# Order of a sum and a remainder, place of a bias load, of three normalisations and of an epsilon in a one-layer attention kernel

## The chip, the cores and the metric

The kernel runs on one core of one Trainium2 chip. A core has TensorE (PE; its weight loads are shown apart, as PEld), VectorE (DVE), ScalarE (ACT), GpSimd (POOL) and SyncE (SP), which here issues nearly all DMA transfers. The engines run side by side, each through its own instructions in a fixed order, and wait for each other by semaphores. The metric is the device time of one execution in microseconds, as the median of several runs.

## The reference

One layer of a streaming encoder, for a sequence of 1024 rows of width 1024, in float32. All matrices are real inputs; nothing is constant.

```python
mod = silu(c) @ w_ada + b_ada                      # shift, scale and gate, each 1024 wide
u = layer_norm(x) * (1 + scale) + shift
h = u @ w_in                                       # q, k, v, g of 8 FoX heads and of 8 stick-breaking heads, ff
log_f = log_sigmoid(ff + b_f);  f_cum = cumsum(log_f, axis=1)
# FoX heads: causal softmax(q k^T / 8 + f_cum[q] - f_cum[k]) @ v
# stick-breaking heads, strictly causal: exp(log_sigmoid(z) + sum of later log_sigmoid(-z)) @ v, z = q k^T / 8
y = concat(fox * silu(fg), sb * silu(sg)) @ w_out
resid = 2 ** 0.25 * x + gate * y
out = layer_norm(resid) * ln_g + ln_b              # epsilon 1e-5 in both norms
```

## The kernel before

Each factor of a product is split into a high half, rounded to TensorE's fast float32 type, and a low half, the remainder. A product is then three: high by high, low by high and high by low. In names, `hi` and `h` stand for high, `lo` and `l` for low.

The work goes in four stages. **The start** normalises the first four tiles of 128 rows of x, transposes them on PE, applies scale and shift, and multiplies the result with the first weights. **The late round** does the same with the last four row tiles. **Attention** goes through 8 pairs of heads with 16 units each (2 heads by 8 query blocks of 128 rows). The projections of the next pairs are spread between the units on PE. **The output** multiplies with `w_out` and normalises again, tile by tile.

Tile's scheduler sets the order of an engine by a simulated time, except where the code fixes it: PE and SP run in program order in the start (`tc.manual_schedule`), PE also afterwards. `after(...)` lets the instructions in its block be ordered only behind a given one, which sets an order and no wait. Buffers come from pools: a pool tag has a number of buffers, and a tile that asks for one waits until all users of the earlier tile in it are done. Tags that matter here: `att` (6 buffers: x_0 to x_5, then the gate weights `wg`, then attention's tiles), `ptl` (3: at first the weights `hw_5`, `hw_6`, `hw_7` of the start, later low halves of attention weights), `T` (2 PSUM banks, for transposes and short products) and `acc`, `pv`, `fl` for accumulators.

In the start, `kb` counts 8 blocks of 128 columns of x. For each, VectorE forms the scale and the shift from 512 KB of `w_ada` (`mod_term(kb, i)`, one sum for i = 0 and one for i = 1, each a product with row sums into `modc`). PE transposes (`u_turn`). ScalarE forms the high half (`u_high`) and the full value, in place in PSUM (`u_full`). VectorE forms the remainder `ul` (`u_rest`). The transposed block 1 lies in the bank that later accumulates `st_k1` (`acc0[NW]`); the others lie in a bank of their own, `xT_early`. The loads of w_ada have three buffers, so the load of block kb + 3 waits for the second sum of block kb. The weights of the start are split by ScalarE (high, `whi_st`) and POOL (low, `wlo_st`); both halves of a block must be there before PE multiplies with it.

`norm_stats(t)` takes mean and variance of row tile t on VectorE, and on POOL adds epsilon and raises to the power -1/2 (`ln_finish`). `norm_x(t)` then normalises in place, on ScalarE for t up to 5 and on VectorE for 6 and 7. Tiles 4 to 7 are first used by the transposes of `late_round(0)`.

`v_first(t, acc)` computes tile t of the v projection of pairs 0 and 1, in 24 products. ScalarE then copies two high halves out of PSUM and VectorE subtracts for the two low ones (`v_tile`). Tiles 0 and 2 use the two halves of one PSUM tile, `late_acc` (`st_late` in the trace), so the first product of tile 2 waits for the copies of tile 0.

The gate vector is `silu(c) @ w_ada` for the third part: POOL multiplies and adds eight loads `wg` in 16 halves (`gate_term`), and `gen_gate` sums over the partitions on PE, one product pair for each half of 512 columns into a `T` bank. VectorE adds the bias `bg`, which is loaded as one row repeated over all 128 partitions. `gen_gate` runs among the fillers of the first attention units, and its T banks alternate with those of attention's transposes (`T_0_0_0`, `T_0_0_1`).

In the output, `o_half` collects a row tile's sum and statistics; the last tile (`OUT_ORDER[-1]`, tile 1) does so in three pieces. After the last statistics, VectorE normalises columns 0 to 832, while POOL, ScalarE, POOL and VectorE in turn treat columns 832 to 1024.

Of the kernel before, what the change touches and what calls it, by code (L numbers as in the profile page):

```python
# [8 lines left out]
F32 = mybir.dt.float32  # L9
# [18 lines left out]
def tile_hybrid_layer(  # L28
# [27 lines left out]
    def att_tile(name, dt=F32):  # L56
        return big("att", 6, name, dt)
# [105 lines left out]
        nc.tensor.matmul(sc_all[:, kt // 4, kt % 4 * P:][:, :P], sc[:, kt:kt + 1].to_broadcast([P, P]), ident,  # L163
                         start=True, stop=True)

    powed = [None]

    def ln_finish(st, name):
        mv = sb.tile([P, 2], F32, tag="mv", bufs=3, name=f"mv_{name}")
        nc.vector.bn_aggr(mv, st)  # L170
        rs = sb.tile([P, 2], F32, tag="rs", bufs=3, name=f"rs_{name}")
        nc.gpsimd.tensor_scalar_add(rs[:, 0:1], mv[:, 1:2], EPS)
        powed[0] = nc.gpsimd.tensor_tensor(rs[:, 0:1], rs[:, 0:1], mhalf, op=ALU.pow)
        return mv, rs

    def ln_stats(src, name):
        st = sb.tile([P, 3, 6], F32, tag="st", bufs=3, name=f"st_{name}")[:, :2, :]
        nc.vector.bn_stats(st[:, 0, :], src[:, 0:512])
        nc.vector.bn_stats(st[:, 1, :], src[:, 512:1024])
        return ln_finish(st, name)  # L180
# [7 lines left out]

    def norm_stats(t):
        mv, rs = norm[t] = ln_stats(xt[t], f"a{t}")  # L190
        if t not in NORM_ON:
            nc.gpsimd.tensor_scalar(rs[:, 1:2], mv[:, 0:1], rs[:, 0:1], -1.0, op0=ALU.mult, op1=ALU.mult)

# [117 lines left out]
    def make_v(g):  # L311
        for p in (2 * g, 2 * g + 1):
            vt[p] = sb.tile([P, NB, 256], F32R, tag="v", bufs=3, name=f"v_{p}")

    def v_tile(g, t, acc, quarters):
        n = 264 if g == 1 else 256
        ts_ = slice(t * P, (t + 1) * P)
        for kt in range(NB):
            hi, lo = quarters[kt // 2]
            s = slice((kt % 2) * n, (kt % 2) * n + n)  # L320
            nc.tensor.matmul(acc[:, :n], u_hi[kt][:, ts_], hi[:, s], start=(kt == 0), stop=False)  # L321
            nc.tensor.matmul(acc[:, :n], u_lo[kt][:, ts_], hi[:, s], start=False, stop=False)  # L322
            nc.tensor.matmul(acc[:, :n], u_hi[kt][:, ts_], lo[:, s], start=False, stop=(kt == NB - 1))  # L323
            if kt == 3:
                yield
        for i in range(2):
            v4 = vt[2 * g + i].rearrange("p t (x c) -> p t x c", c=HD)
            a4 = acc[:, i * P:(i + 1) * P].rearrange("p (x c) -> p x c", c=HD)
            nc.scalar.copy(v4[:, t, 0::2, :], a4)
            nc.vector.tensor_tensor(v4[:, t, 1::2, :], a4, v4.bitcast(F32)[:, t, 0::2, :],  # L330
                                    op=ALU.subtract)
        if g == 1:
            nc.vector.tensor_tensor(fsb[:, :, t], acc[:, 256:264], bf_sb, op=ALU.add)
        yield
# [321 lines left out]
    for kb in range(NB):  # L656
        last = kb == NB - 1
        if last:
            start_steps(ALL[:2], acc0, kb)
            for n in range(2):  # L660
                evac_m(*START[n], 0, acc0[n])
            start_steps(ALL[2:], acc0, kb)
            break
        start_steps(ALL[:4], acc0, kb, parts=(0,))
        u_turn(kb + 1, tp=xt_early if kb else acc0[NW])
        with after(split_at["k", kb + 1][0]):
            high = u_high(kb + 1)
        if kb == 0:
            with after(high):
                start_split(("h", 0))  # L670
            high = split_at["h", 0][0]
        with after(high):
            u_full(kb + 1)
        sums = [mod_term(kb + 2, i) for i in range(2 if kb == 0 else 1)] if kb + 2 < NB else []
        with after(*sums):
            rest = u_rest(kb + 1)
        if 0 < kb < NB - 2:
            with after(rest):
                mod_term(kb + 2, 1)
        if kb == 0:  # L680
            start_steps(ALL[:4], acc0, kb, parts=(1,))
        else:
            if kb == 1:
                start_steps(ALL[4:], acc0, 0)
            start_steps(ALL[4:], acc0, kb, parts=(0,))
            start_steps(ALL, acc0, kb, parts=(1,))
        if kb + 2 < NB:
            start_split(("k", kb + 2))
        if kb == 2:
            start_split(("h", 1))  # L690
        if kb + 5 < NB:
            load_ss(kb + 5)
            if kb == 0:
                load_w4(6, 2)
        if kb == 2:
            for n in range(2):
                v0_load(n)
            load_x(4)
            for n in range(2, 4):
                v0_load(n)  # L700
            for t in range(5, NB):
                load_x(t)
        if kb == 5:
            with after(*split_at["k", NB - 1]):
                for n in range(4):
                    v0_split(n)
            norm_stats(4)
            norm_stats(5)
            norm_x(4)
            norm_x(5)  # L710
        if kb == 6:
            with after(rest):
                for t in (6, 7):
                    norm_stats(t)
                    norm_x(t)
            make_v(0)

    wg = {}
# [11 lines left out]
            nc.gpsimd.tensor_tensor(gate[:, s], gate[:, s], wg[kt][:, s], op=ALU.add)  # L730

    def gen_gate():
        b = att_tile("bg")
        nc.sync.dma_start(b, b_gate.to_broadcast([P, D]))
        parts = [pt_tile(0, f"gate_{x}") for x in range(2)]
        nc.scalar.copy(parts[0], gate)
        nc.gpsimd.tensor_tensor(parts[1], gate, parts[0].bitcast(F32), op=ALU.subtract)
        for _ in range(GATE):
            yield
        for h in range(2):  # L740
            s = slice(h * 512, h * 512 + 512)
            gp = t_tile(f"gate_{h}")
            for part in range(2):
                nc.tensor.matmul(gp, half.to_broadcast([P, P]), parts[part][:, s], start=(part == 0), stop=(part == 1))
            nc.vector.scalar_tensor_tensor(gate[:, s], b[:, s], 0.5, gp, op0=ALU.mult, op1=ALU.add)
            yield

    def late_round(kb):
# [7 lines left out]
    def v_first(t, acc):  # L756
        for _ in v_tile(0, t, acc, v0_w):
            pass

    v_first(0, late_acc[:, 0, :])  # L760
    v_first(1, t_tile("v_0_1"))
    v_first(2, late_acc[:, 1, :])
    late_round(0)
# [4 lines left out]
    for kb in range(NB):  # L768
        if kb + 2 < NB:
            rounded = late_round(kb + 2)  # L770
        start_steps(range(2), acc1, kb, 512, 1024)
        if kb < 4:
            load_gate(kb)
            gate_term(kb, 0)
            gate_term(kb, 1)
        if kb == 3:
            v0_w.update((n, fetch_w(f"v0_{n}b", w_v[0, n], 512)) for n in (2, 3))
            for kt in range(4, NB):
                load_gate(kt)
                gate_term(kt, 0)  # L780
                gate_term(kt, 1)
        if kb < len(evacs):
            n, h = evacs[kb]
            with after(*rounded):
                evac_m(*START[n], 0, acc0[n], (h,))
# [95 lines left out]
    def o_half(t, h):  # L881
# [3 lines left out]
        if h == 0:  # L885
# [4 lines left out]
        nc.vector.scalar_tensor_tensor(r[:, s], xr[:, s], ALPHA, o_acc[t, h][:, :s.stop - s.start],  # L890
                                       op0=ALU.mult, op1=ALU.add)
        nc.vector.bn_stats(st[:, h, :], r[:, s])
        if h == ng - 1:
            mv, rs = ln_finish(st, f"b{t}")
            cuts = ((0, 512), (512, 832)) if t == OUT_ORDER[-1] else ((0, 512), (512, 1024))
            for a, b in cuts:
                gain, bias = ((ps_ln[i][a // 512][:, :b - a] for i in range(2)) if ps_ln else
                              (lgb[0][:, i, a:b] for i in range(2)))
                nc.vector.scalar_tensor_tensor(r[:, a:b], r[:, a:b], mv[:, 0:1], gain,
                                               op0=ALU.subtract, op1=ALU.mult)  # L900
                nc.vector.scalar_tensor_tensor(r[:, a:b], r[:, a:b], rs[:, 0:1], bias,
                                               op0=ALU.mult, op1=ALU.add)
                nc.sync.dma_start(out[ts_, a:b], r[:, a:b])
            if t == OUT_ORDER[-1]:
                e = slice(832, 1024)
                nc.gpsimd.tensor_scalar(rs[:, 1:2], mv[:, 0:1], rs[:, 0:1], -1.0, op0=ALU.mult, op1=ALU.mult)
                nc.scalar.activation(r[:, e], r[:, e], AF.Identity, scale=rs[:, 0:1], bias=rs[:, 1:2])
                nc.gpsimd.tensor_tensor(r[:, e], r[:, e], lgb[0][:, 0, e], op=ALU.mult)
                nc.vector.tensor_tensor(r[:, e], r[:, e], ps_ln[1][1][:, 832 - 512:], op=ALU.add)
                nc.sync.dma_start(out[ts_, e], r[:, e])  # L910
# [183 lines left out]
```

## Time and profile before

| | |
|---|---|
| median of 3 runs | 686.94 us (686.88 to 687.93) |
| profiled execution | 687.67 us |
| its span, first to last instruction | 685.9 us |
| PE busy | 668.6 us, 97% of the span |
| DVE busy | 450.2 us, 66% |
| POOL busy | 427.0 us, 62% |
| ACT busy | 381.5 us, 56% |
| granted TensorE clock, mean | 0.998 of full speed |

The profile is of one execution. A timeline row gives the start in us, the duration in us, the engine, the line of the kernel, the operation, what it writes and reads by the program's names without numbers, the shape, and how often it came in a row. In square brackets stands the time that the engine stood idle just before, and what ended that. SPq is a transfer's issue on SP's queue, not the transfer. Matmul ends are modelled, so the start of the next one tells more than the end of the last. In the list of waits a row names who waited, for whom, the total in us, how often, and the longest.

### The profile page before, as it was taken

The numbers are of one execution on the slowest core, as the hardware profiler recorded it, in microseconds if no ns is written. First come the engines' busy times: TensorE is split into PE (matmuls) and PEld (weight loads), VectorE is DVE, ScalarE is ACT, GpSimd is POOL, SyncE is SP. The second block draws the span as 40 slices with busy tenths as digits, with TensorE's granted clock in tenths as the row PEclk, the third lists the DMA queues.
The fourth block names the chain that finished last, engine by engine and source line by source line (L and its number), as shares of the span: only waits on it lengthen the run. The fifth ranks groups of instructions, "written<-read, shape, count | busy, mean of one in ns | idle before, by whom it ended". The sixth has DMA issues, their size and how long they took to land.

```text
span 685.9 us, 11768 instructions
## 1 busy us (share of the span) xinstructions
PE 668.6 (97%) x4021; PEld 587.9 (86%) x4021; DVE 450.2 (66%) x914; ACT 381.5 (56%) x861; POOL 427.0 (62%) x558
## 2 busy tenths in 40 slices
PE   5999999999999999999999999999999999999996
PEld 4788888888998888889998888889988889888885
DVE  6785348767666676676675665666565767774645
ACT  5577447856667666575674564655565666531000
POOL 5558967656448665556388897877584364665411
PEclk9999999999999999999999999999999999999999
DMA  9966241012102111112144554454351288143301
GB/s 338 410 224 240 62 124 43 25 40 54 40 9 72 39 55 55 38 50 60 35 137 142 177 162 121 151 151 142 105 146 43 65 328 321 57 156 122 125 31 62
DMA packets 45036, 81.60 MB, mean 119 GB/s; under 512 B 5232, under 2 KB 18864, under 8 KB 44976
## 3 DMA queue, kind: packets, MB, share of 16 engines
q1 hardware_dynamic: 43536, 76.63, 34.2%
q10 hardware_dynamic: 1440, 4.21, 2.0%
q8 instruction: 32, 0.52, 0.3%
q14 instruction: 28, 0.23, 0.1%
HBM read 60.34 MB, written 16.29 MB: 112 GB/s over the span
## 4 chain that ended last, share of the span: by engine, by line
PE 85%; POOL 6%; DMA 4%; issue 2%; DVE 2%; ACT 1%; SPq 0%; POOLq 0%; DVEq 0%
PE m L266 10%; PE pv L487 10%; PE m L267 10%; PE m L268 10%; PE T L472 9%; PE S L422 5%; PE S L421 5%; PE o L877 4%; PE o L875 4%; PE o L876 4%; PE v L321 4%; PE v L322 4%; PE v L323 4%; POOL gate L730 2%; POOL wg L729 1%
## 5 line engine op out<-in xcount | busy, mean ns | idle before, releaser
L266 PE MATMUL m<-uh,whi 128*128 128x512 f32 x304 | 126.5, 416 | 0.0
L268 PE MATMUL m<-uh,wlo 128*128 128x512 f32 x304 | 119.8, 394 | 0.0
L267 PE MATMUL m<-ul,whi 128*128 128x512 f32 x304 | 119.8, 394 | 0.0
L475 DVE TENSOR_TENSOR pt<-T,pt 128x512 fp32r<-128x512 f32 (+2 forms) x192 | 100.5, 550 | 17.9 <-ACT pt L474 16.9
L455 POOL TENSOR_TENSOR be<-be,kp 128x127 f32<-128x127 f32 (+3 forms) x64 | 77.1, 1206 | 35.4 <-DVE kp L451 23.5
L474 ACT CAST pt<-T 128x512 fp32r<-128x512 f32 (+2 forms) x192 | 85.7, 480 | 16.0 <-PE T L472 12.3
L447 DVE TENSOR_TENSOR_SCAN kp<-kp,floor 128x512 f32<-128x512 f32 (+2 forms) x64 | 65.2, 1018 | 30.9 <-ACT kp L441 30.0
L487 PEld LDWEIGHTS pv<-pt,v 128*128 128x128 f32 (+1 forms) x640 | 77.2, 163 | 4.5 <-DVE pt L475 0.7
L487 PE MATMUL pv<-pt,v 128*128 128x256 f32 (+3 forms) x640 | 80.4, 272 | 0.5 <-DVE pt L475 0.5
L436 POOL TENSOR_SCALAR a<-a,l 128x1024 f32<-128x1024 f32 (+3 forms) x64 | 47.9, 749 | 39.6 <-DVE l L435 28.6
L434 ACT ACTIVATE a<-a,nm 128x1024 f32<-128x1024 f32 (+3 forms) x64 | 49.8, 778 | 34.5 <-DVE nm L428 33.4
L268 PEld LDWEIGHTS m<-uh,wlo 128*128 128x128 f32 x304 | 57.2, 188 | 13.5
L421 PE MATMUL S<-k,q 128*128 128x512 f32 (+5 forms) x192 | 66.6, 348 | 0.2 <-DVE nm L428 0.2
L422 PE MATMUL S<-kl,qz 128*128 128x512 f32 (+5 forms) x192 | 65.5, 343 | 0.0
L266 PEld LDWEIGHTS m<-uh,whi 128*128 128x128 f32 x304 | 57.4, 189 | 8.5 <-DVE kl L254 0.2
L267 PEld LDWEIGHTS m<-ul,whi 128*128 128x128 f32 x304 | 57.5, 189 | 7.9
L428 DVE CUSTOM_DVE_ANT_0 a<-S,fb 128x1024 f32<-128x1024 f32 (+3 forms) x64 | 48.3, 755 | 20.4 <-PE S L422 8.9
L508 POOL TENSOR_TENSOR ty<-ty,sg 64x256 f32<-64x256 f32 x64 | 47.5, 742 | 22.6 <-DVE ty L507 11.5
L441 ACT ACTIVATE kp<-S 128x128 f32<-128x128 f32 (+3 forms) x64 | 41.7, 651 | 31.7 <-PE S L422 28.4
L321 PE MATMUL v<-whi_v,uh 128*128 128x256 f32 (+1 forms) x192 | 56.1, 292 | 0.0
L399 ACT CAST qz<-q 64x128 fp32r<-64x128 f32 x128 | 37.4, 295 | 32.8 <-PE S L422 31.6
L322 PE MATMUL v<-whi_v,ul 128*128 128x256 f32 (+1 forms) x192 | 54.3, 283 | 0.0
(283 smaller groups left out, 1594.2 us busy)
## 6 DMA issues: line engine op xcount, KB each, us to landing
raw<-in_w_qkg_dram SPq DMA_DIRECT2D x38, 256.0 KB, 2.8
wss<-in_w_ss_dram SPq DMA_DIRECT2D x16, 512.0 KB, 8.4
x<-in_x_dram SPq DMA_DIRECT2D x8, 512.0 KB, 6.9
k<-k SPq DMA_DIRECT2D x32, 128.0 KB, 2.3
wg<-in_w_gate_dram SPq DMA_DIRECT2D x8, 512.0 KB, 4.6
raw_o<-in_w_out_dram SPq DMA_DIRECT2D x16, 256.0 KB, 3.0
fb<-f_dr ACTq DMA_DIRECT2D x8, 512.0 KB, 4.2
wo_dr<-whi_o SPq DMA_DIRECT2D x16, 256.0 KB, 2.8
```

What stands on the lines that cost most here:

```text
L266: nc.tensor.matmul(acc, hi[:, c], u_hi[kt][:, s], start=(kt == 0), stop=False)
L267: nc.tensor.matmul(acc, hi[:, c], u_lo[kt][:, s], start=False, stop=False)
L268: nc.tensor.matmul(acc, lo[:, c], u_hi[kt][:, s], start=False, stop=(kt == NB - 1))
L321: nc.tensor.matmul(acc[:, :n], u_hi[kt][:, ts_], hi[:, s], start=(kt == 0), stop=False)
L322: nc.tensor.matmul(acc[:, :n], u_lo[kt][:, ts_], hi[:, s], start=False, stop=False)
L421: nc.tensor.matmul(S[:, s, :w], qst[p][h][:, qs], kst[p][h][:, ks], start=True, stop=False)
L422: nc.tensor.matmul(S[:, s, :w], z, klo[p][:, ks], start=False, stop=True)
L447: scan = nc.vector.tensor_tensor_scan(rv, rv, floor[0][:, 512 - n:][:, ::-1], initial=0.0, op0=ALU.mult, op1=ALU.max)
L455: nc.gpsimd.tensor_tensor(be[:, :ke - 1], be[:, :ke - 1], kp[:, 1:ke], op=ALU.mult)
L474: nc.scalar.copy(hi[:, :n, qo:qo + P], t3)
L475: nc.vector.tensor_tensor(lo[:, :n, qo:qo + P], t3, hi.bitcast(F32)[:, :n, qo:qo + P], op=ALU.subtract)
L487: nc.tensor.matmul(acc[:m, q0:256], vt[p][:, kb, h * P:h * P + m], pt[:, kb % 4, q0:], start=start, stop=stop)
```

## The change

It makes four edits.

1. At block 0 of the start, VectorE forms the remainder of block 1 between the two sums of block 2, as it did at the later blocks (first sum, remainder, second sum). At block 6 the remainder is ordered behind the joined statistics of row tile 4.
2. `norm_x` of row tiles 5, 6 and 7 is ordered behind the copies of the first v tile.
3. The gate bias is loaded behind the last gate weights, in a buffer of the tag `ptl` instead of `att`.
4. At the last output tile, epsilon is added to the first piece's statistics (to its sum of squares, times 1024), and no more to the variance after the last piece.

```diff
-    powed = [None]
+    powed, joined = [None], {}
-    def ln_finish(st, name):
+    def ln_finish(st, name, with_eps=False):
         mv = sb.tile([P, 2], F32, tag="mv", bufs=3, name=f"mv_{name}")
-        nc.vector.bn_aggr(mv, st)
+        joined["last"] = nc.vector.bn_aggr(mv, st)
         rs = sb.tile([P, 2], F32, tag="rs", bufs=3, name=f"rs_{name}")
-        nc.gpsimd.tensor_scalar_add(rs[:, 0:1], mv[:, 1:2], EPS)
-        powed[0] = nc.gpsimd.tensor_tensor(rs[:, 0:1], rs[:, 0:1], mhalf, op=ALU.pow)
+        var = mv[:, 1:2]
+        if not with_eps:
+            var = rs[:, 0:1]
+            nc.gpsimd.tensor_scalar_add(var, mv[:, 1:2], EPS)
+        powed[0] = nc.gpsimd.tensor_tensor(rs[:, 0:1], var, mhalf, op=ALU.pow)
...
         mv, rs = norm[t] = ln_stats(xt[t], f"a{t}")
+        joined[t] = joined.pop("last")
...
-            nc.scalar.copy(v4[:, t, 0::2, :], a4)
-            nc.vector.tensor_tensor(v4[:, t, 1::2, :], a4, v4.bitcast(F32)[:, t, 0::2, :],
-                                    op=ALU.subtract)
+            v_last[:] = [nc.scalar.copy(v4[:, t, 0::2, :], a4),
+                         nc.vector.tensor_tensor(v4[:, t, 1::2, :], a4, v4.bitcast(F32)[:, t, 0::2, :],
+                                                 op=ALU.subtract)]
...
-        sums = [mod_term(kb + 2, i) for i in range(2 if kb == 0 else 1)] if kb + 2 < NB else []
+        sums = [mod_term(kb + 2, 0)] if kb + 2 < NB else [joined[4]]
         with after(*sums):
             rest = u_rest(kb + 1)
-        if 0 < kb < NB - 2:
+        if kb + 2 < NB:
             with after(rest):
                 mod_term(kb + 2, 1)
...
             norm_x(4)
-            norm_x(5)
         if kb == 6:
             with after(rest):
                 for t in (6, 7):
                     norm_stats(t)
-                    norm_x(t)
...
     def gen_gate():
-        b = att_tile("bg")
-        nc.sync.dma_start(b, b_gate.to_broadcast([P, D]))
...
-            nc.vector.scalar_tensor_tensor(gate[:, s], b[:, s], 0.5, gp, op0=ALU.mult, op1=ALU.add)
+            nc.vector.scalar_tensor_tensor(gate[:, s], bg[:, s], 0.5, gp, op0=ALU.mult, op1=ALU.add)
...
     v_first(0, late_acc[:, 0, :])
+    with after(*v_last):
+        for t in (5, 6, 7):
+            norm_x(t)
...
                 load_gate(kt)
                 gate_term(kt, 0)
                 gate_term(kt, 1)
+            bg = pt_tile(1, "bg", F32)
+            nc.sync.dma_start(bg, b_gate.to_broadcast([P, D]))
...
+        final = t == OUT_ORDER[-1]
+        if final and h == 0:
+            nc.gpsimd.tensor_scalar_add(st[:, 0, 2:3], st[:, 0, 2:3], EPS * D)
         if h == ng - 1:
-            mv, rs = ln_finish(st, f"b{t}")
+            mv, rs = ln_finish(st, f"b{t}", with_eps=final)
```

VectorE, in the start around the remainder of block 1 (`ISA` with `wss_2` is a sum of block 2 and its second row the read of the row sums, `ul_1` the remainder). Before:

```order
L203 ISA wss_2_161,modc_128<-sc_all_103,wss_2_161,bss_sb_98 128x1024
L203 ISA modc_128 128x1
L203 ISA wss_2_161,modc_128<-sc_all_103,wss_2_161,bss_sb_98 128x1024
L203 ISA modc_128 128x1
L228 TENSOR_TENSOR ul_1_121<-st_k1_140,uh_1_113 128x512
L203 ISA wss_3_211,modc_128<-sc_all_103,wss_3_211,bss_sb_98 128x1024
```

and now:

```order
L207 ISA wss_2_161,modc_128<-sc_all_103,wss_2_161,bss_sb_98 128x1024
L207 ISA modc_128 128x1
L232 TENSOR_TENSOR ul_1_121<-st_k1_140,uh_1_113 128x512
L207 ISA wss_2_161,modc_128<-sc_all_103,wss_2_161,bss_sb_98 128x1024
L207 ISA modc_128 128x1
L207 ISA wss_3_211,modc_128<-sc_all_103,wss_3_211,bss_sb_98 128x1024
```

The remainder has moved ahead of the second sum.

VectorE, from the end of the start to the second v tile (`v_0`, `v_1` from `st_late` are the copies of the first v tile, from `v_0_1` those of the second; `x_6`, `x_7` the normalisations; `kl` belongs to k). Before:

```order
L250 TENSOR_TENSOR kl_0_242<-st_k0_137,k_0_1_241 64x512
L170 BN_AGGR mv_a7_510<-st_a7_507 128x2
L330 TENSOR_TENSOR v_0_516<-st_late_544,v_0_516 128x2x64
L198 TENSOR_SCALAR x_6_363<-x_6_363,mv_a6_501,rs_a6_503 128x1024
L330 TENSOR_TENSOR v_1_517<-st_late_544,v_1_517 128x2x64
L330 TENSOR_TENSOR v_0_516<-v_0_1_573,v_0_516 128x2x64
L198 TENSOR_SCALAR x_7_365<-x_7_365,mv_a7_510,rs_a7_512 128x1024
L330 TENSOR_TENSOR v_1_517<-v_0_1_573,v_1_517 128x2x64
```

and now:

```order
L254 TENSOR_TENSOR kl_0_242<-st_k0_137,k_0_1_241 64x512
L336 TENSOR_TENSOR v_0_513<-st_late_541,v_0_513 128x2x64
L170 BN_AGGR mv_a7_508<-st_a7_505 128x2
L336 TENSOR_TENSOR v_1_514<-st_late_541,v_1_514 128x2x64
L202 TENSOR_SCALAR x_6_363<-x_6_363,mv_a6_500,rs_a6_502 128x1024
L202 TENSOR_SCALAR x_7_365<-x_7_365,mv_a7_508,rs_a7_510 128x1024
L336 TENSOR_TENSOR v_0_513<-v_0_1_573,v_0_513 128x2x64
L336 TENSOR_TENSOR v_1_514<-v_0_1_573,v_1_514 128x2x64
```

Both copies of the first v tile stand ahead of x_6 and x_7, and both of the second behind. On ScalarE `x_5` has moved in the same way from ahead of the two casts of the first v tile to behind them.

SP, from the last gate weights to the first attention units (`wg` gate weights, `k` the half-copies of k, `raw` weights). Before:

```order
L722 DMA wg_7_789<-in_w_gate_dram 128x1024
L248 DMA k_1_0_245<-k_1_0_245 64x512
L248 DMA k_1_1_246<-k_1_1_246 64x512
L248 DMA k_0_0_240<-k_0_0_240 64x512
L248 DMA k_0_1_241<-k_0_1_241 64x512
L121 DMA raw_1_2_0_1228<-in_w_qkg_dram 128x512
L121 DMA raw_1_2_1_1234<-in_w_qkg_dram 128x512
L248 DMA k_1_0_245<-k_1_0_245 64x512
L121 DMA raw_2_0_0_1557<-in_w_qkg_dram 128x512
L734 DMA bg_958<-in_b_gate_dram 128x1024
L248 DMA k_1_1_246<-k_1_1_246 64x512
L797 DMA bf_sb_941<-in_b_f_dram 128x8
```

and now:

```order
L726 DMA wg_7_789<-in_w_gate_dram 128x1024
L788 DMA bg_795<-in_b_gate_dram 128x1024
L252 DMA k_1_0_245<-k_1_0_245 64x512
L252 DMA k_1_1_246<-k_1_1_246 64x512
L252 DMA k_0_0_240<-k_0_0_240 64x512
L252 DMA k_0_1_241<-k_0_1_241 64x512
L121 DMA raw_1_2_0_1228<-in_w_qkg_dram 128x512
L121 DMA raw_1_2_1_1234<-in_w_qkg_dram 128x512
L252 DMA k_1_0_245<-k_1_0_245 64x512
L121 DMA raw_2_0_0_1557<-in_w_qkg_dram 128x512
L252 DMA k_1_1_246<-k_1_1_246 64x512
L804 DMA bf_sb_943<-in_b_f_dram 128x8
```

bg has moved from behind the weights of `raw_2_0_0` to right behind the last gate weights, past eight transfers. Two other pairs have changed places by themselves: on VectorE the joined statistics of tile 4 stand ahead of the remainder of block 7, and on POOL the rounding of the last v weights stands ahead of the last sum of the gate. At the end POOL has lost one step of 128x1 behind the last statistics and has one more ahead of them. Everything else stands as it did.

More of the change, by code (lines that the diff above doesn't have):

```diff
@@ L313, in make_v @@
             vt[p] = sb.tile([P, NB, 256], F32R, tag="v", bufs=3, name=f"v_{p}")
+    v_last = []
     def v_tile(g, t, acc, quarters):
```

## Prediction

> **What bounds the kernel now.** I read the page first, then PE's part of the waits, then the timeline around each wait that the diff touches. The page gives the busy time and, in its fourth part, the chain that ended last, by engine:
>
> ```profile
> span 685.9 us, 11768 instructions
> ...
> PE 668.6 (97%) x4021; PEld 587.9 (86%) x4021; DVE 450.2 (66%) x914; ACT 381.5 (56%) x861; POOL 427.0 (62%) x558
> ...
> PE 85%; POOL 6%; DMA 4%; issue 2%; DVE 2%; ACT 1%; SPq 0%; POOLq 0%; DVEq 0%
> ```
>
> PE is busy for 668.6 of 685.9 us and carries most of the chain. No other engine is above 66%. So the time changes only where PE's few gaps change, or behind PE's last product. The waits of PE, longest first, of nine rows the four that matter here:
>
> ```profile
> PE gate L744 <- DVE gate L745: 0.8, 1, 0.8
> PE T L472 <- DVE pt L475: 0.8, 1, 0.8
> ...
> PE st_k L583 <- DVE ul L228: 0.5, 1, 0.5
> ...
> PE st_late L321 <- DVE v L330: 0.2, 1, 0.2
> ```
>
> Three of them lie at lines that the diff moves: the second bias product of the gate, the first product into st_k, and the third v tile. The T row lies right behind them and is not touched. Between the last of these and the final tile PE runs almost without a gap and the order of every engine is as before, so time won in front should arrive at the end as it is.
>
> **Edit 1, order at block 0.** PE may not write st_k before VectorE has taken ul from it, since that bank served as scratch for the transposed block 1. The stretch:
>
> ```profile
> 18.10 0.75 ACT L221 ACTIVATE st_k<-st_k,modc 128x512 f32<-128x512 f32 x1
> ...
> 18.88 1.28 DVE L203 CUSTOM_DVE_ANT_0 wss<-sc_all,wss,bss_sb 128x1024 f32<-128x1024 f32 x1
> ...
> 20.09 0.69 DVE L228 TENSOR_TENSOR ul<-st_k,uh 128x512 fp32r<-128x512 f32 x1
> ...
> 20.82 0.19 PEld L583 LDWEIGHTS st_k<-uh,whi_st 128*128 128x128 f32 x1 [0.77 <-DVE ul L228]
> ...
> 20.92 0.62 ACT L569 CAST whi_st<-raws 128x512 fp32r<-128x512 f32 x1 [2.07 <-DMA raws<-in_w_qkg_dram]
> ...
> 21.62 1.30 POOL L571 TENSOR_TENSOR wlo_st<-raws,whi_st 128x512 fp32r<-128x512 f32 x1 [2.05 <-ACT whi_st L569]
> ...
> 23.26 0.19 PEld L583 LDWEIGHTS st_q<-uh,wlo_st 128*128 128x128 f32 x1
> ```
>
> ScalarE is done with st_k at 18.85. VectorE then runs the second sum of block 2 for 1.28 us before ul. With the two exchanged, ul ends near 19.57, and the weight load that waited 0.77 us need not wait. The sum ends about 0.6 later, near 20.8. Its reader, the rounding of block 2, comes behind the cast of 20.92 to 21.54 on ScalarE, which waits for weights from memory, so this costs nothing while that load is no faster. SP also waits for that sum before it reloads the buffer, and so sends two loads and the 512 KB behind them 0.6 us later. Their users are sums two and a half blocks on, behind which VectorE stands idle for ScalarE; I take that as hidden.
>
> The 0.77 is not kept. The low halves of block 2's weights are made by 22.92 (21.62 and 1.30) from the same load, which does not move. PE loads them at 23.26. With the 0.04 us that passed between ul's end (20.78) and PE's load, PE can come forward by 23.26 - 22.92 - 0.04 = 0.30 us and no more. The ends are 0 (that load later) and 0.77 (earlier); I take **0.30**, the nearest row.
>
> The join of tile 4's statistics ahead of ul at block 6 falls into a gap in which VectorE waits for ScalarE. Its follower on POOL stands behind a weight split there, in the same order as before. I take 0, and it costs nothing either.
>
> **Edit 2, the last x tiles behind the first v tile.** Here are the first v tile's products, the third's, and what lies between:
>
> ```profile
> 49.19 0.29 PE L323 MATMUL st_late<-v_w,uh 128*128 128x256 f32 x1
> 49.31 0.28 PE L321 MATMUL v<-v_home,uh 128*128 128x256 f32 x1
> ...
> 49.71 1.24 ACT L199 ACTIVATE x<-x,rs_a 128x1024 f32<-128x1024 f32 x1
> 49.82 0.69 DVE L250 TENSOR_TENSOR kl<-st_k,k 64x512 fp32r<-64x512 f32 x1
> ...
> 50.98 0.27 ACT L329 CAST v<-st_late 128x128 fp32r<-128x128 f32 x1
> ...
> 52.06 0.29 PE L323 MATMUL v<-v_w,uh 128*128 128x256 f32 x1
> 52.20 0.28 DVE L330 TENSOR_TENSOR v<-st_late,v 128x128 fp32r<-128x128 f32 x1
> ...
> 52.54 0.39 PE L321 MATMUL st_late<-v_home,uh 128*128 128x256 f32 x1 [0.20 <-DVE v L330]
> ...
> 52.89 0.80 DVE L198 TENSOR_SCALAR x<-x,mv_a,rs_a 128x1024 f32<-128x1024 f32 x1
> ...
> 55.51 1.03 PE L211 MATMUL xT<-ident,x 128*128 128x128 f32 x8
> ```
>
> Products of this size start 0.12 apart (49.19, 49.31). The third tile's first would follow at 52.18 and starts at 52.54, when the second copy out of the first tile (52.20 to 52.48) is done: 0.36 us lost. What delays that copy is x_5's normalisation on ScalarE (1.24 us) ahead of the casts, and x_6's on VectorE. With both moved behind, ScalarE casts at 49.71, VectorE is free at 50.51, and the four short steps of about 0.28 with their handovers end near 51.4, about 0.8 before PE asks. So **0.36**, ends 0 and 0.36. Against it stands what is late next: x_5, x_6 and x_7 start behind that and end by about 53.2, with some 0.5 more if POOL's power for x_7 is slow. x_7 ended at 53.69 until now and the transposes want it at 55.51 less the 0.66 that PE gained. The copies of the second v tile move behind x_7 too, to about 54, and the second four transposes need their buffer near 55.2. Both are covered, by some 1 us.
>
> **Edit 3, the gate bias with the gate weights.** The bias load, the two bias products and what stands behind them:
>
> ```profile
> 81.89 0.40 PE L586 MATMUL st_q1b<-ul,hw 128*128 128x512 f32 x1
> ...
> 85.34 1.58 SPq L121 DMA_DIRECT2D raw<-in_w_qkg_dram  x2
> ...
> 91.90 0.45 SPq L734 DMA_DIRECT2D bg<-in_b_gate_dram  x1
> ...
> 93.22 0.41 POOL L455 TENSOR_TENSOR be<-be,kp 128x127 f32<-128x127 f32 x1 [0.42 <-DVE kp L447]
> ...
> 94.59 0.62 PE L744 MATMUL gate<-gate,half 128*128 128x512 f32 x2
> ...
> 95.39 0.27 PE L472 MATMUL T<-ident,be 128*128 128x128 f32 x1
> ...
> 96.83 0.28 PE L323 MATMUL v<-wlo_v_3b,uh 128*128 128x256 f32 x1
> ...
> 97.18 0.69 DVE L745 SCALAR_TENSOR_TENSOR gate<-bg,gate 128x512 f32<-128x512 f32 x1 [2.47 <-PE v L323]
> ...
> 97.92 0.73 PE L744 MATMUL gate<-gate,half 128*128 128x512 f32 x2 [0.81 <-DVE gate L745]
> ```
>
> The first bias product is done at 95.21, yet VectorE adds the bias only at 97.18, 5.28 us after SP issued the load of bg. (The row blames PE's v, which is a product VectorE doesn't read there.) PE's second bias product needs one of the two T buffers, which the first holds. It would follow the product of 96.83 at 96.95 and starts at 97.92: **0.97** us, of which none is left once bg is there in time. VectorE then stands 1.9 us earlier at the scan, and the next T buffer comes free earlier as well.
>
> When is bg there? Its new place is a buffer of the low-weight pool, which has three, all held by start-up weights. The oldest is the one for block 4 (hw), last read for st_q1b at 81.89. SP reaches bg before that and stands there until the next product starts, 0.24 later, less the 0.66 won: 81.5. With the 5.28 bg lands near 87, and 7 us are left. Behind it in SP's queue stand four half-copies of k and the weight loads of the next g tile. At 0.45 an issue the copies leave by 83.7. The copies are read only by later scores (the fifth query block of the pair and on), and the weight loads waited until 85.34 for their buffer anyway. POOL's last gate sum and a weight rounding (0.6) change places, which delays only the gate's rounding, and that is ready well ahead of the first bias product. That is why I take the whole 0.97; the lower end is 0.
>
> **Edit 4, epsilon early at the last tile.** The end of the kernel:
>
> ```profile
> 680.41 0.22 POOL L172 TENSOR_SCALAR rs_b<-mv_b 128x1 f32<-128x1 f32 x1 [9.85 <-DVE mv_b L170]
> 680.72 0.57 POOL L173 TENSOR_TENSOR rs_b<-rs_b,mhalf 128x1 f32<-128x1 f32 x1
> ...
> 681.49 1.20 DVE L901 SCALAR_TENSOR_TENSOR r<-r,rs_b,ps_bias 128x512 f32<-128x512 f32 x2
> ...
> 682.94 0.35 DVE L909 TENSOR_TENSOR r<-r,ps_bias 128x192 f32<-128x192 f32 x1 [0.26 <-POOL r L908]
> ```
>
> Without the addition the power starts 0.31 earlier (680.41 instead of 680.72). The added step runs while POOL is idle for 9.85 us. The last addition, which ends the output, waits 0.26 for POOL's chain, then VectorE's own queue (busy to 682.69) holds it. So **0.26**, ends 0 and 0.31. [...]
>
> **The sum.** 0.30 + 0.36 + 0.97 + 0.26 = 1.89 us off the profiled execution: its span of 685.9 becomes 684.0 and its 687.67 us 685.8. The median of the three runs is 686.94, 0.73 below that execution; 1.89 off gives 685.05, and I say 685.0.
>
> **The rivals.** First, PE keeps more of edit 1, because the weights of block 2 come early enough: 0.47 more, 684.6. The 2.07 us that ScalarE waited for them speak against it. Second, what PE wins in front is taken up again behind: the T wait stands here:
>
> ```profile
> 111.62 0.63 PE L472 MATMUL T<-ident,be 128*128 128x128 f32 x4 [0.77 <-DVE pt L475]
> ```
>
> If VectorE's chain up to it did not move with PE, up to 1.63 us would go into a longer wait there, and the time would be between 685.6 and 686.7. Against it, up to there ScalarE and POOL wait for PE and VectorE again and again, so they follow.
>
> Third, the other sign: SP stands too long in front of bg. If bg got the buffer that is read last,
>
> ```profile
> 89.62 0.39 PE L586 MATMUL st_k1b<-ul,hw 128*128 128x512 f32 x1
> ```
>
> bg would leave near 89.2, and the second of the weight loads, six issues of 0.45 behind it, at 91.9 instead of 86.5. POOL splits those weights ahead of its be product at 93.22, whose transposition PE wants 0.66 earlier than 95.39, at 94.73; be ends at 93.63 less 0.30. With POOL's 0.42 idle that leaves 1.8, so of the 5.4 us 3.6 would be lost: 688.6. It begins to cost when bg leaves after 85.6 and makes the kernel slower than before from 87.5 on. Fourth, one of the small edits brings nothing (x_7 late, or the final addition held elsewhere): 685.4.
>
> **How the numbers follow.** The forecast has 0.55, with 684.5 to 685.5 as its own range; more of edit 1 has 0.10, the gain taken up behind 0.20, SP's queue 0.05, a small edit without effect 0.10. A change below 0.2% (1.37 us, so a time above 685.57) can't be told from none here. Faster by more: most of the forecast (0.51), 0.10, most of the fourth (0.07) and a little of the second, 0.70. Slower by more: 0.05. The rest is 0.25. The range goes from 684.2 (the first rival and the runs' scatter) to 686.7 (all taken up).
>
> **What would show it.** Right: among PE's waits the rows of gate, st_k and st_late are gone or replaced by one of some 0.4 for wlo_st near 22.7; SP issues bg near 81.5; VectorE adds the first bias near 94.6; the last addition follows its queue without a wait. Wrong: a new wait of PE for be or T near 94, a T row longer than 0.8, or transposes that wait for x_7 near 55, bg issued past 85.

## The result, and the profile after

The changed kernel takes 685.25 us (median of 9 runs, 685.02 to 685.34), the kernel before in the same comparison 687.76 us (9 runs). The ratio is 0.996 with a 95% interval of 0.9947 to 0.9972, so the change is a gain of 0.3 to 0.5%. Predicted were 685.0 us, with a range of 684.2 to 686.7. Among the experiments below, one execution of edit 3 alone (2350.16 us) and one with the last write from ScalarE (945.9 us) lie far outside all others and are left out of the medians and ratios.

The profiled executions differ by 2.42 us (687.67 and 685.25), as their spans do (685.9 and 683.5). The page of the changed kernel, its first line and the first of its fourth part:

```profile
span 683.5 us, 11770 instructions
...
PE 94%; DMA 3%; DVE 2%; ACT 0%; issue 0%; POOL 0%; DVEq 0%
```

PE's share of the chain rose from 85% to 94%, and POOL's 6% went. PE's waits in the changed kernel, all of them:

```profile
PE sc_all L163 <- POOL later L313: 5.4, 1, 5.4
PE st_q L589 <- ACT uh L220: 1.1, 1, 1.1
PE xT_early L215 <- ACT x L203: 1.1, 2, 0.6
PE T L478 <- DVE pt L481: 0.8, 1, 0.8
PE pv L493 <- DVE pt L481: 0.5, 1, 0.5
PE S L427 <- DVE nm L434: 0.2, 1, 0.2
```

The rows of gate, st_k and st_late are gone. The T row stands at 0.8 as before. Both waits for xT_early lie in the start, before 12.5 us, and none near 55. PE's order of instructions is the same in both kernels, so its products can be paired one by one, and the start of each in the one trace taken from its start in the other gives PE's lead. From the first product of the start on, the lead changes by more than a tenth only at these places (starts in us; the last column is the change at the place, so small drifts between two rows are not in it):

| product | before | changed | lead | what the edit left |
|---|---|---|---|---|
| first of the start, ahead of every edit | 14.14 | 13.90 | 0.24 | |
| the one behind the first product with block 2's wlo_st (edit 1) | 23.72 | 23.06 | 0.66 | 0.42 |
| second of the third v tile (edit 2) | 52.76 | 51.67 | 1.09 | 0.46 |
| T behind the second bias product (edit 3) | 99.06 | 96.80 | 2.26 | 1.18 |
| a T product late in attention | 582.07 | 579.64 | 2.43 | 0.18 with the products behind it |
| last product | 678.86 | 676.37 | 2.49 | |
| end of the span | 685.95 | 683.53 | 2.42 | -0.07 (edit 4) |

The 0.24 ahead of every edit is no part of the change. The kernel with edit 4 alone, which is the kernel before up to the last tile, leads by 0.22 there too, and all eleven experiments lead by 0.22 to 0.44: the one profiled execution of the kernel before began late. The rest is 2.17 us, of which 1.99 stand at the four edits; 1.89 were predicted for them.

**Edit 1.** The changed kernel's timeline in the start:

```profile
18.64 0.69 DVE L232 TENSOR_TENSOR ul<-st_k,uh 128x512 fp32r<-128x512 f32 x1
...
19.80 0.48 PE L589 MATMUL st_k<-uh,whi_st 128*128 128x512 f32 x1
...
20.68 0.62 ACT L575 CAST whi_st<-raws 128x512 fp32r<-128x512 f32 x1 [2.07 <-DMA raws<-in_w_qkg_dram]
...
21.37 1.29 POOL L577 TENSOR_TENSOR wlo_st<-raws,whi_st 128x512 fp32r<-128x512 f32 x1 [2.05 <-ACT whi_st L575]
...
22.71 0.19 PEld L589 LDWEIGHTS st_q<-uh,wlo_st 128*128 128x128 f32 x1 [0.50 <-POOL wlo_st L577]
22.71 0.51 PE L589 MATMUL st_q<-uh,wlo_st 128*128 128x512 f32 x1
23.06 0.39 PE L589 MATMUL st_k<-uh,whi_st 128*128 128x512 f32 x1
```

The first product into st_k comes at 19.80 without a wait, which is 0.78 beyond the lead that PE had. The next product with low halves of block 2 stood at 23.49 before. At 22.71 the weight load waits for the low halves, which are made from 21.37 to 22.66.

**Edit 2.** The copies of the first v tile, the normalisations behind them, the third v tile's first two products and the first transposes of the last tiles:

```profile
49.08 0.27 ACT L335 CAST v<-st_late 128x128 fp32r<-128x128 f32 x1
...
50.53 0.29 DVE L336 TENSOR_TENSOR v<-st_late,v 128x128 fp32r<-128x128 f32 x1 [0.22 <-ACT v L335]
50.74 1.69 DVE L202 TENSOR_SCALAR x<-x,mv_a,rs_a 128x1024 f32<-128x1024 f32 x2
...
51.56 0.28 PE L327 MATMUL st_late<-v_home,uh 128*128 128x256 f32 x1
51.67 0.28 PE L328 MATMUL st_late<-v_home,ul 128*128 128x256 f32 x1
...
54.43 1.04 PE L215 MATMUL xT<-ident,x 128*128 128x128 f32 x8
```

The second copy ends at 50.82, 0.74 ahead of PE's product at 51.56. x_7 ends at 52.43, 2 us ahead of the transposes.

**Edit 3.** The bias load, the first addition of the bias and the second bias product:

```profile
81.25 0.33 SPq L788 DMA_DIRECT2D bg<-in_b_gate_dram  x1
...
94.17 0.69 DVE L747 SCALAR_TENSOR_TENSOR gate<-bg,gate 128x512 f32<-128x512 f32 x1 [0.54 <-PE gate L746]
...
95.87 0.63 PE L746 MATMUL gate<-gate,half 128*128 128x512 f32 x2
...
109.33 0.84 PE L478 MATMUL T<-ident,be 128*128 128x128 f32 x6 [0.83 <-DVE pt L481]
```

VectorE now waits for the bias product and no more for the load. The T row behind it stood at 111.62 before with a wait of 0.77: it moved by 2.29 with a wait of 0.83.

**Edit 4.** The end:

```profile
676.37 0.28 PE L884 MATMUL o<-wol,y7h 128*128 128x256 f32 x1
...
677.14 0.43 DVE L899 BATCH_NORM_STATS2 st_b<-r 128x6 f32<-128x256 f32 x1
677.67 0.23 DVE L170 BATCH_NORM_AGGREGATE mv_b<-st_b 128x2 f32<-128x18 f32 x1
...
679.60 0.59 POOL L919 TENSOR_TENSOR r<-r,lngb 128x192 f32<-128x192 f32 x1 [0.66 <-ACT r L918]
679.84 0.81 SPq L914 DMA_DIRECT2D out_dram<-r  x2
680.22 0.35 DVE L920 TENSOR_TENSOR r<-r,ps_bias 128x192 f32<-128x192 f32 x1
680.74 0.41 SPq L921 DMA_DIRECT2D out_dram<-r  x1
```

The last addition has no wait any more, yet the span ends 7.16 us after the start of PE's last product, against 7.09 before.

### The profile page after: what moved, and what is told of

Same layout as the page of the kernel before. It is cut to its first block, busy times and chain, and to the rows that moved or that the text cites. A ratio compares the mean times of both kernels' runs of the same rounds, so it can differ in the third digit from the quotient of the medians.

```text
span 683.5 us, 11770 instructions
## 1 busy us (share of the span) xinstructions
PE 667.2 (98%) x4021; PEld 587.2 (86%) x4021; DVE 450.6 (66%) x914; ACT 382.0 (56%) x861; POOL 427.7 (63%) x558
## 4 chain that ended last, share of the span: by engine, by line
PE 94%; DMA 3%; DVE 2%; ACT 0%; issue 0%; POOL 0%; DVEq 0%
PE m L270 10%; PE m L272 10%; PE m L271 10%; PE pv L493 10%; PE T L478 9%; PE S L428 5%; PE S L427 5%; PE o L884 4%; PE o L882 4%; PE o L883 4%; PE v L327 4%; PE v L328 4%; PE v L329 4%; DMA raws<-in_w_qkg_dram 2%; PE st_late L589 1%; PE st_q L589 1%
## 5 line engine op out<-in xcount | busy, mean ns | idle before, releaser
L480 ACT CAST pt<-T 128x512 fp32r<-128x512 f32 (+2 forms) x192 | 85.8, 480 | 16.1 <-PE T L478 12.5
```

The lines of the kernel that those rows point to most:

```text
L480: nc.scalar.copy(hi[:, :n, qo:qo + P], t3)
```

## Experiments

Each is compared with runs of the kernel before on the same chip. "End" is the time from the start of PE's last product to the end of the span.

| kernel | median us (n) | before | ratio, 95% interval | end |
|---|---|---|---|---|
| edit 1 alone | 686.84 (11) | 687.42 | 0.9989, 0.998 to 0.9998 | 7.09 |
| edit 2 alone | 685.52 (6) | 687.42 | 0.9971, 0.996 to 0.9982 | 7.10 |
| edit 3 alone | 686.05 (10) | 687.42 | 0.9978, 0.9969 to 0.9987 | 7.09 |
| edit 4 alone | 687.42 (11) | 687.42 | 0.9998, 0.9989 to 1.0007 | 7.17 |
| changed, weights of block 2 earlier | 684.94 (5) | 687.48 | 0.9966, 0.9954 to 0.9979 | 7.16 |
| changed, steps alternating at the end | 685.25 (5) | 687.48 | 0.9969, 0.9956 to 0.9981 | 7.35 |
| the same without edit 4 | 685.27 (6) | 687.48 | 0.9969, 0.9957 to 0.9981 | 7.39 |
| changed, last write from ScalarE | 685.14 (5) | 687.48 | 0.9968, 0.9955 to 0.998 | 7.15 |
| changed kernel again | 685.14 (6) | 687.32 | 0.9968, 0.9957 to 0.998 | 7.16 |
| changed without edit 3 | 685.53 (10) | 687.32 | 0.9975, 0.9966 to 0.9984 | 7.15 |
| changed without edit 4, weights of block 2 earlier | 684.74 (5) | 687.32 | 0.9961, 0.9947 to 0.9975 | 7.09 |

Many of the intervals overlap. What tells the kernels apart is mostly the step of the lead at each place, which repeats closely: in all nine kernels with edit 2, its step is 0.46.

### One edit at a time

Each kernel is the kernel before with the lines of one edit from the diff above. Edit 1 alone:

> Edit 1 alone on the kernel before. As the two traces read: PE starts the first product into st_k 0.8 us earlier (0.77 of wait), then waits about 0.25 for the low halves of block 2's weights and starts again 0.1 slower, so 0.40 of it is left behind 25 us and at the end. As predicted: 0.30. Rival (the weights are early enough on their own): 0.77. The other rows of PE's waits (gate 0.8, st_late 0.2) stay.

The lead rose by 0.42 at edit 1, as in the changed kernel, and by another 0.32 at the gate, where the load of the bias came somewhat sooner (its row: 0.5 instead of 0.8):

```profile
PE gate L745 <- DVE gate L746: 0.5, 1, 0.5
```

Edit 2 alone:

> Edit 2 alone. As the two traces read: the row of st_late goes, PE is 0.36 earlier at the third v tile and another 0.11 at the product behind it, because PE doesn't start anew after a wait: 0.47. As predicted: 0.36. Rival (x_7 or a copy becomes late): a new wait of PE near 55 and less than 0.2.

Here the expectation failed by far, on the good side. The step of 0.46 at the third v tile is there, but so is the whole 1.18 at the gate, which edit 2 was not meant to touch. PE has seven rows of waits, among them the row of st_k, and none of gate:

```profile
...
PE T L474 <- DVE pt L477: 0.9, 1, 0.9
PE st_k L585 <- DVE ul L228: 0.6, 1, 0.6
...
```

The reason stands in SP's rows:

```profile
89.90 0.47 SPq L248 DMA_DIRECT2D k<-k  x1
90.41 0.58 SPq L734 DMA_DIRECT2D bg<-in_b_gate_dram  x1
91.90 0.33 SPq L121 DMA_DIRECT2D raw<-in_w_qkg_dram  x1
```

In the kernel before, one weight load stands ahead of bg in SP's queue; with edit 2 the scheduler puts bg ahead of that load. So it left at 90.41, 1.49 earlier than before. VectorE still waits 1.2 us for it and adds the bias at 95.1, and that is early enough for PE. Edit 1 alone gives PE the same lead up to there (0.73, against 0.75 here) and keeps the wait: there bg left at 91.06 and the bias was added at 96.1. So at the same lead of PE, the load's issue 0.65 us sooner, and its landing 4.6 us behind the issue instead of 5.0, made the difference. A kernel below, without edit 3 but with edit 2, shows the same order and no wait either.

Edit 3 alone:

> Edit 3 alone. As the two traces read: 0.97 at the second bias product and twice 0.1 behind it, 1.18 in all. As predicted: 0.97. Rival (taken up behind): the wait for pt near 111 grows from 0.77 by about 1. If the late load of the bias is also what spreads the runs of the kernel before (686.9 to 688.2), the runs of this one lie within 0.5 us; if the spread comes from the start, as wide as before.

The step at the gate is 1.18, and the wait for pt near 111 stays at 0.8, so nothing is taken up behind. The expectation that the runs lie within 0.5 us did not hold: they lie between 685.77 and 686.47, which is 0.70. Edits 1 and 4 alone, which keep the late load, spread no more than 0.83, so that load is not shown to spread the runs.

Edit 4 alone:

> Edit 4 alone. From PE's last product to the end of the span the kernel before takes 7.09 us. As predicted: 0.26 less, 6.83. As the trace of the changed kernel reads (7.16 with the last addition's wait gone): no gain, 7.05 to 7.20, since the end follows the first of the three output writes by 2.27 us, with the DMA engines full, and that write doesn't move.

No gain: the median is that of the kernel before, and the end takes 7.17 us. The interval alone would still allow the prediction's 0.26 us (0.04%); the trace excludes it. It has the last addition 0.23 earlier after PE's last product (3.85 instead of 4.08) and the end 0.08 later.

### What holds the end

Which resource takes edit 4's gain? The last of the three output writes sent by ScalarE:

```diff
-                nc.sync.dma_start(out[ts_, e], r[:, e])
+                nc.scalar.dma_start(out[ts_, e], r[:, e])
```

> The changed kernel, with the last of the three output writes issued by ScalarE, which is idle, instead of SP, which issues the two before it until 0.09 us ahead. If SP's queue is what took edit 4's gain: 0.13 less to the end, 7.03. If the DMA engines, full with the two writes before, took it: 7.16, no change.

The write was issued earlier, at 680.35, which is 4.23 after PE's last product instead of 4.37. The end did not move (7.15). The DMA engines are the limit. Their busy share from the first packet to the last, first of the changed kernel, then of this one (each row has the stretch and its length; the last two columns are the DMA share, where 1.00 is all 16 engines busy, and GB/s; the others do not matter here):

```profile
680.64:681.32 0.68, 0.00 (x0) 1.00 0.95 370
681.32:681.88 0.56, 0.00 (x0) 0.65 1.05 374
681.88:682.16 0.28, 0.00 (x0) 0.50 0.69 225
```

```profile
680.38:681.06 0.68, 0.00 (x0) 0.00 (x0) 0.00 (x0) 0.00 (x0) 0.00 (x0) 0.50 0.95 370
681.06:681.62 0.56, 0.00 (x0) 0.00 (x0) 0.00 (x0) 0.00 (x0) 0.00 (x0) 0.50 1.05 374
681.62:681.91 0.29, 0.00 (x0) 0.00 (x0) 0.00 (x0) 0.00 (x0) 0.00 (x0) 0.50 0.67 217
```

The three writes are 512 KB, and they take 1.52 us without a gap, at 370 GB/s until the last 0.3 us; in the kernel before it is 1.55 us, from 683.05 to 684.60. The earlier last write only queued behind the two before it: its packets, which are known by their size of 768 bytes, begin 5.37 after PE's last product in the changed kernel and in this one alike. The write was issued 0.14 us sooner (4.23 instead of 4.37), and none of it reached the packets.

Then an earlier first write should help, and VectorE's four steps were put in turn (product, bias, product, bias):

```diff
+            first = []
             for a, b in cuts:
...
-                nc.vector.scalar_tensor_tensor(r[:, a:b], r[:, a:b], mv[:, 0:1], gain,
+                with after(*first):
+                    nc.vector.scalar_tensor_tensor(r[:, a:b], r[:, a:b], mv[:, 0:1], gain,
...
-                nc.vector.scalar_tensor_tensor(r[:, a:b], r[:, a:b], rs[:, 0:1], bias,
+                one = nc.vector.scalar_tensor_tensor(r[:, a:b], r[:, a:b], rs[:, 0:1], bias,
...
+                first = [one] if t == OUT_ORDER[-1] else []
```

> The changed kernel, with VectorE's four steps of the last tile in the order product, bias, product, bias, so that the first output write leaves 0.45 us earlier, while the last addition comes some 0.1 later. If the three writes set the end: about 0.2 less from PE's last product to the end, 6.9 to 7.0 instead of 7.16. Rival (the last addition sets it): 0.1 more, 7.26.

Worse than either theory: 7.35. The first write did leave earlier, 3.21 after PE's last product instead of 3.47. But the second (4.25 instead of 3.92) and the third came later, and a gap opened between the packets:

```profile
678.59 0.75 DVE L914 SCALAR_TENSOR_TENSOR r<-r,rs_b,ps_bias 128x512 f32<-128x512 f32 x1
...
679.25 0.54 DVE L912 SCALAR_TENSOR_TENSOR r<-r,mv_b,ps_gain 128x320 f32<-128x320 f32 x1
679.36 1.37 SPq L917 DMA_DIRECT2D out_dram<-r  x2
...
680.83 0.38 SPq L924 DMA_DIRECT2D out_dram<-r  x1
```

```profile
680.16:680.96 0.80, 0.00 (x0) 0.00 (x0) 0.48 (x2) 0.00 (x0) 0.00 (x0) 0.50 0.85 328
680.96:681.20 0.24, 0.00 (x0) 0.00 (x0) 0.00 (x0) 0.00 (x0) 0.00 (x0) 0.50 0.00 0
681.20:681.80 0.60, 0.00 (x0) 0.00 (x0) 0.00 (x0) 0.00 (x0) 0.00 (x0) 0.50 0.80 294
```

From the first of the four steps to the last addition VectorE took 2.57 us instead of 2.28, since each bias step now starts behind the end of the product just before it (0.11 and 0.04 us behind). SP sent the last write 4.68 after PE's last product instead of 4.37. So both count here: the first write starts the transfer, and the second, issued at 680.40, began at 681.20, 0.80 behind its issue like the first (679.36 to 680.16), when the first had been through for 0.24. In the order of the changed kernel no gap opened.

> The same order at the last tile, without edit 4. The bias step then waits for the power, 0.31 later. If the writes set the end, edit 4 is worth 0.2 to 0.3 here, though alone it is worth nothing: 7.15 to 7.25 from PE's last product to the end. If edit 4 is worth the same everywhere: by the prediction 0.26, by the two traces 0.

Without edit 4 the same order gives 7.39. Edit 4 is worth 0.04 here, not the 0.2 to 0.3 expected. With it the power is ready 2.19 after PE's last product instead of 2.43, but the first bias step starts only at 2.43 instead of 2.46, since it now waits for VectorE's own product, which ends at 2.32.

### What holds edit 1

```diff
-    def load_w1(h):
-        raw = start_raw(1)
+    def load_w1(h, raw=None):
+        raw = start_raw(1) if raw is None else raw
...
-    load_w1(1)
+    raw_h1 = start_raw(1)
     load_w4(2, 2)
+    load_w1(1, raw_h1)
```

> The changed kernel, with the load of the weights of blocks 2 and 3 issued ahead of the second quarter of the later weight (its 256 KB are 0.6 us at the 410 GB/s of that stretch). If those weights are what kept edit 1 from its full 0.77: PE's wait of 0.50 for wlo_st near 22.7 goes, PE is 0.25 + 0.12 = 0.37 earlier behind 25 us and at the end. Rival (another operand, u_hi of block 2, is as late): a wait of about the same length in its place and less than 0.1.

PE's wait for wlo_st is gone, and the step at edit 1 is 0.78 instead of 0.42. But this trace doesn't settle the question. In this profiled execution PE lost 1.2 us ahead of it, because its granted clock was 0.50 for 3.4 us (shown in the last section), and PE so late finds everything ready. Edit 3 alone, late in the same way, has a step of 0.78 at st_k without edit 1, and the changed kernel without edit 3, late too, has no wait for wlo_st with the weights loaded as before. The last kernel below has the full clock there (1.00 in every stretch from 13 to 24), and it shows that the weights are the limit.

### Edit 3 beside edit 2, and a faster kernel

> The changed kernel itself, unchanged, for the two beside it: 685.0 to 685.4 by all theories, 7.16 us from PE's last product to the end.

It repeats: 685.14 us, the same steps, an end of 7.16.

```diff
-            bg = pt_tile(1, "bg", F32)
-            nc.sync.dma_start(bg, b_gate.to_broadcast([P, D]))
...
     def gen_gate():
+        b = att_tile("bg")
+        nc.sync.dma_start(b, b_gate.to_broadcast([P, D]))
```

> The changed kernel without edit 3: the gate bias is loaded again where it was. With edit 2 in it, the order of SP puts that load one weight load earlier than in the kernel before. If that is enough for PE, as edit 2 alone showed (issued at 90.4, VectorE waits 1.2 us for it, PE not at all): no row of gate among PE's waits and the time of the changed kernel, 685.0 to 685.6. If edit 3 is worth what the prediction gave it: 0.97 to 1.18 slower, 686.2 to 686.5.

The step at the gate is 0.99 without edit 3, and 1.18 with it. PE has no row of gate, though VectorE waits for the load:

```profile
95.69 0.69 DVE L749 SCALAR_TENSOR_TENSOR gate<-bg,gate 128x512 f32<-128x512 f32 x1 [1.48 <-DMA bg<-in_b_gate_dram]
```

So beside edit 2, edit 3 adds 0.19 us. It goes without any idle time of PE: the weight load of the second bias product waits for the addition and starts at 96.43, 0.02 ahead of its product, where the changed kernel has 0.12 (95.75 and 95.87), and the products behind come later by 0.1 twice. The median is 0.39 above the changed kernel's beside it; this profiled execution, too, had the granted clock at 0.50 in the start, and a mean granted clock of 0.995. Without the runs with that mean (two here, one there) the difference is 0.35, so the clock explains little of it. The runs of the two kernels overlap, and what stands behind the rest stays open.

The last kernel takes the changed one, loads the weights of block 2 earlier, as above, and leaves edit 4 out:

> The changed kernel without edit 4 and with the weights of blocks 2 and 3 loaded ahead of the second quarter of the later weight. If the readings of the runs before hold: 0.37 less at the start and 0.07 less at the end (7.09 from the last product to the end), 684.8. If the clock and not the order of the loads made that run faster, no more than 0.07: 685.2.

It is the fastest: 684.74 us, all five runs between 684.56 and 684.76, where the six of the changed kernel beside it begin at 684.87 and have 685.14 as their median. The 0.40 between the medians was expected as 0.44. The step at edit 1 is 0.78, and the end takes 7.09:

```profile
20.02 1.14 ACT L575 CAST whi_st<-raws 128x512 fp32r<-128x512 f32 x2 [1.43 <-DMA raws<-in_w_qkg_dram]
...
20.72 2.55 POOL L577 TENSOR_TENSOR wlo_st<-raws,whi_st 128x512 fp32r<-128x512 f32 x2 [1.41 <-ACT whi_st L575]
...
22.44 0.40 PE L589 MATMUL st_q<-uh,wlo_st 128*128 128x512 f32 x1
22.68 0.39 PE L589 MATMUL st_k<-uh,whi_st 128*128 128x512 f32 x1
```

The cast comes 0.66 earlier than in the changed kernel, and PE goes through at 22.44 without a wait.

## Why the prediction was right, point by point

The time and the sum came out near (1.89 predicted, 1.99 found at the four edits), but not each term. Three were somewhat too small and one was wrong, and these nearly cancelled. That the time itself came within 0.25 us is partly luck, too: it was reckoned from a median of 686.94 of three runs, and the nine runs beside the changed kernel gave 687.76, 0.82 more, while the gain came out at 2.51 instead of 1.89. In the traces, 0.24 of the gain stand ahead of every edit and 0.18 near 582, which no term has. The sum taken from 687.76 would have said 685.87, still inside the range.

- **Edit 1, 0.30 predicted, 0.42 found.** The mechanism held: the wait for st_k went, and a wait for wlo_st took its place, at 22.71, as forecast near 22.7. The term was mis-sized because it was taken between weight loads. The load ran ahead of its product where PE was busy (23.26 and 23.49 before), but not where PE waited (22.71 for both). So PE could come forward by 23.49 - 22.92 - 0.05 = 0.52 (22.92 is the end of the low halves before, 0.05 the time from their end to the load now), and lost 0.11 again where it started anew. The first rival (0.77 kept) needs the weights earlier; with them earlier 0.78 was kept.
- **Edit 2, 0.36 predicted, 0.46 found.** Right, and x_7, expected by about 53.2, was no danger at 52.43. The 0.1 more is that the product behind the waiting one came 0.22 after it before, and now 0.11. What the term lacked altogether is edit 2's effect on SP's order, by which it removes the gate's wait too.
- **Edit 3, 0.97 predicted, 1.18 found.** The load left at 81.25 (predicted 81.5) and the addition came at 94.17 (predicted 94.6). The 0.21 more is again the start behind a wait, at two places of 0.1. But "its worth" depends on what stands beside it: 1.18 alone, 0.19 beside edit 2. The sum over the four edits was right because the wait was counted once.
- **Edit 4, 0.26 predicted, -0.07 found.** This step failed. The rows were read rightly up to the last addition: from the joined statistics to POOL's last product it takes 1.93 us instead of 2.23. That is 0.30 less, so the spacing of the starts (0.31) was the better measure of POOL's step than its span (0.22). The error came behind it: the last addition was taken for the end, and the writes behind it, which keep the DMA engines full (busy share 0.94 and 1.01 before, until the last 0.3 us), were left out of the sum. Their end hangs on the first write, and that one on VectorE's first bias step, which POOL did not hold up before either: the power was ready 2.43 after PE's last product, and VectorE's own product kept that step until 2.63. The -0.07 is a new wait: joining the statistics now also waits for POOL's early addition, and starts 0.53 after the start of the last statistics step instead of 0.46, in all seven kernels with edit 4 and in none of the six without. VectorE's steps and the first write follow 0.07 later.
- **The rivals.** The gain was not taken up behind: the T row stayed, and the lead grew by 0.18 near 582. That step appears in every kernel in which the gate's wait is gone and in no other; what in the chain carries it that far was not followed, and stays open. SP's queue was not blocked, since bg left at 81.25; a later buffer was not tried. That one small edit brings nothing was a rival with 0.10, and it is what happened, but its time (685.4) assumed that the other terms were exact.

## What to carry to other kernels

Follow a wait to the transfer behind it, at the end of a kernel above all: here the last addition ended at 680.57, and the span, with the writes behind it, at 683.53. When several edits move instructions under a scheduler, time each alone and also leave each out, since one edit may shift another's transfer in a queue, as edit 2 did with the bias. And when a wait is removed, look up what the freed engine asks for next: here the next weights, whose loads only had to change places.

## What the runs showed of the hardware

**Two waits cost PE about 0.1 us beyond their idle time.** Where edits 2 and 3 removed a wait, the product behind came about 0.1 us sooner as well: 52.54 to 52.76 before and 51.56 to 51.67 now at the third v tile, 97.92 to 98.49 before and 95.87 to 96.34 now at the gate. Behind the first product into st_k it did not (0.33 and 0.32); there the product follows transposes in both kernels.

**A wait for work long done cost 0.07 us.** POOL's early addition started at 672.56, 5.1 us before the statistics were joined, and yet the join, which waits for it since, starts 0.07 later.

**PE's granted clock fell to half in the start of three of the eleven traces of experiments**, in kernels with different edits. A stretch of edit 3 alone (granted clock in the third column from the right):

```profile
15.40:18.20 2.80, 2.80 (x10) 2.28 (x9) 2.00 (x3) 1.45 (x3) 1.27 (x1) 0.50 1.02 413
```

```profile
17.56 0.63 PE L586 MATMUL st_k<-ul,whi_st 128*128 128x512 f32 x1
17.99 0.63 PE L586 MATMUL st_g<-ul,whi_st 128*128 128x512 f32 x1
```

The products start 0.43 apart there and 0.23 otherwise. In all three traces the clock is at 0.50 for 3.4 us (from 15.26 to 18.67 with edit 3 alone). It cost 1.2 us with edit 3 alone, of which that kernel got 0.78 back, because PE then came late enough for st_k and had nothing to wait for. What made the clock fall is not shown. From 13 to 15 us PE was busy for 1.12, 1.24 and 1.31 us in these three traces, and for 0.86 to 1.29 us in nine others, where the clock stayed at 1.00 from 13 to 24.
